# The down projection of an encoder's MLP by Strassen's scheme, its weight differences on GpSimd

## The chip, the cores and the metric

The kernel runs on one core of a Trainium2 chip. A core has five engines that run side by side, each with its own queue of instructions in a fixed order: TensorE (PE) multiplies matrices, VectorE (DVE), ScalarE (ACT) and GpSimd (POOL) work elementwise, SyncE (SP) issues transfers. The metric is the device time of one execution in microseconds, as the median of several runs. Operands lie in SBUF, the matmuls' sums in PSUM, which has eight banks of 128 x 512 fp32 numbers.

## The reference

Two layers of an encoder on 512 tokens of width 1024. Each layer has a token mixer (two kinds of attention, gated and projected) and then an MLP:

```
mod = silu(c) @ ada_w[l] + ada_b[l]            # 6 x 1024 numbers: shifts, scales, gates
h = rms_norm(x, norm_mlp_g[l]) * (1.0 + scale_f) + shift_f
x = x + gate_f * (jnp.square(jax.nn.relu(h @ w_mlp_up[l])) @ w_mlp_down[l])
```

The up projection is 1024 to 4096, the down projection 4096 to 1024. All is fp32.

## The kernel before

**Precision.** Every fp32 operand is split into a high part, in the matmul's format `fp32r`, and a low part, the rest. A product is three matmuls into the same sum (`mm3`, L265): high by high, high by low, low by high. A weight block of 128 x 1024 comes by DMA into a tile `raw`; `split_w` (L249) makes its high part `wh` on ACT (a copy that rounds) and its low part `wl` on DVE (`raw` minus `wh`). There are four `raw` buffers (`rawp`, L51) and five pairs of `wh` and `wl` (`wp`, L52). Larger tiles of 4 KB a partition share 24 buffers (`bigp`), 512-wide scratch six.

**The MLP.** The hidden 4096 columns are worked on in eight chunks (the loop `for fc`, L965) of four blocks of 128. `up_part` (L946) multiplies one block's weights with the normed activations `hF` for all 512 tokens: 8 x 3 = 24 matmuls of 512 columns into a bank. Then ACT takes the relu `r`, DVE makes the square `q` from the bank and `r`, ACT and DVE split `q` into the two halves of a tile `uT`. After four blocks the chunk's down products follow: for each half `cc` of the 1024 output columns and each of the four token tiles `t`, 4 x 3 = 12 matmuls into a bank; DVE multiplies it with the gate row `gf` into `d`, and POOL adds `d` to the residual tile `x1[t]` (in the last chunk DVE adds). The first three blocks (`EARLY`) are begun ahead of the loop, half of their tokens at a time.

**The conditioning of the next layer.** While layer 0's chunks run, `ada` (L141) forms the 48 blocks of `mod` for layer 1: a 128 x 1024 block of `ada_w` into a `raw` buffer, multiplied with the broadcast `cbc` and summed along its rows by one DVE instruction (profile: `raw<-raw,cbc,colt`). Eight are called behind each of the first six chunks. With `pool_` set, POOL multiplies (`raw<-raw,cbc`), ACT sums, and a small DVE addition (the closure `add`) closes.

**Order.** In the chunk loop no order is written out: a planner sorts the instructions by the order of the program text and by what it takes to be ready, with times that it estimates, and assigns buffers as they come free. On the chip each engine then runs its own list in that order and waits where something isn't ready. In other stages (the last output projection and the beginning of the up blocks, the last half chunk of layer 0, attention) `order(True)` keeps the order of the text.

**Banks.** `acc()` takes PSUM banks in turn from two pools, `accp` (2) and `ssp` (3). Two more (`tpp`) serve transposes, one (`pvp`) attention.

In the profile nearly every instruction has line L81, that of a helper; so groups are told apart by tile names. Names there merge the two parts of a matmul's operands: `acc<-wh,uT` holds high by high and low by high.

Of the kernel before, what the change touches and what calls it, by code (L numbers as in the profile page):

```python
# [10 lines left out]
F32 = mybir.dt.float32  # L11
R32 = mybir.dt.float32r
BF = mybir.dt.bfloat16
I32 = mybir.dt.int32
AF = mybir.ActivationFunctionType
OP = mybir.AluOpType
AX = mybir.AxisListType

DEPTH = 2
# [4 lines left out]
NFF = 32  # L24
FCH = 4
# [16 lines left out]
def trunk(ctx, tc, x, c, pos, cols, rows, ada_w, w_qkv, w_gate, w_ba, w_bb, w_out, w_up, w_down, out):  # L42
# [8 lines left out]
    rawp = pool("raw", 4)  # L51
    wp = pool("w", 5)  # L52
    halfp = pool("half", 10)
    pp = pool("p", 2)
    sp = pool("scr", 2)
    accp = pool("acc", 2, PS)
    ssp = pool("ss", 3, PS)
    tpp = pool("tp", 2, PS)
    pvp = pool("pv", 1, PS)
    dram = pool("dram", 1, bass.MemoryType.DRAM)  # L60

    def nosync(after, before):
        tc.add_manual_dep(after.ins, before.ins.name,
                          mybir.DependencyInfo(mybir.DependencyClass.NoSync,
                                               mybir.DependencyReason.DATA), reason="order")
# [23 lines left out]
    T_, V_, S_, G_ = Ordered(nc.tensor), Ordered(nc.vector), Ordered(nc.scalar), Ordered(nc.gpsimd)  # L89
    E_ = Ordered(nc.sync)  # L90
    matmul = T_.matmul
    transpose = T_.transpose
    big = lambda shape, dt, name: bigp.tile(shape, dt, name=name, tag="big")
    turns = [0]

    def acc(wide=True):
        turns[0] += 1
        if wide and turns[0] % 5 >= 2:
            return ssp.tile([128, 512], F32, name="acc", tag="s")
        return accp.tile([128, 512], F32, name="acc", tag="acc")  # L100
# [40 lines left out]
    def ada(l, j, far=False, pool_=False):  # L141
        raw = big([128, D], F32, "raw") if far else rawp.tile([128, D], F32, name="raw", tag="raw")
        E_.dma_start(raw, ada_w[l, j])
        m, bias = modT[l][:, j:j + 1], adab[l][:, j:j + 1]

        def add():
            S_.activation(raw, raw, AF.Copy, accum_out=m)
            V_.tensor_add(m, m, bias)

        if pool_:  # L150
            G_.tensor_mul(raw, raw, cbc)
            return add
        else:
            ins = V_.tensor_tensor_reduce(raw, raw, cbc, 1.0, bias, OP.mult, OP.add, m)
            if floor[0] is not None:
                nosync(ins, floor[0])
# [105 lines left out]
                                           op0=OP.mult, op1=OP.subtract)  # L262
        return hi, lo

    def mm3(o, sh, sl, mh, ml, start, stop):  # L265
        matmul(o, sh, mh, start=start, stop=False)
        matmul(o, sh, ml, start=False, stop=False)
        matmul(o, sl, mh, start=False, stop=stop)

    def rsq(o, ms):  # L270
        G_.tensor_scalar(ms[:, 0:1], ms[:, 0:1], ms[:, 1:2], EPS, op0=OP.add, op1=OP.add)
# [47 lines left out]
    def affine(l, m):  # L319
        aT = small([128, KT], "aT")  # L320
        sc = modT[l][:, 24 * m + 8:24 * m + 16]
        V_.scalar_tensor_tensor(aT, sc, 1.0, gnorm[l, m], op0=OP.add, op1=OP.mult)
        return aT

    def grow(l, m):
        g = pp.tile([128, D], F32, name="grow", tag="p")
        before = T_.last
        for q in range(2):
            tp = tps()
            for k in range(4):  # L330
                j = 24 * m + 16 + 4 * q + k
                ins = transpose(tp[:, k], modT[l][:, j:j + 1].to_broadcast([128, 128]), ident)
                if before is not None:
                    nosync(ins, before)
            S_.activation(g[:, 512 * q:512 * q + 512], tp.rearrange("p a b -> p (a b)"), AF.Copy)
        return g
# [255 lines left out]
    EARLY = 3  # L592
# [14 lines left out]
    def prepare(l):  # L607
        hT = []
        return hT, [qkv(l, p, int(p < 6), hT) for p in range(NB_Q)]
# [104 lines left out]
    for l in range(DEPTH):  # L714
# [161 lines left out]
        x1 = {}  # L876
        zT = []
        wb = None
        for j in range(KT):
# [11 lines left out]
            wh, wl = split_w(w_ba[l, j], scale=sg[:, l:l + 1])  # L891
# [5 lines left out]
            zb = sp.tile([128, 512], F32, name="zb", tag="f512", bufs=6)  # L897
# [12 lines left out]
        up = {}  # L910
        ms = {}
        for cc in range(2):
            w = [split_w(w_out[l, cc, i], spare=cc == 1 and i == 0) for i in range(4)]
# [5 lines left out]
            for t in range(NT):  # L919
                if cc == 0:  # L920
                    x1[t] = load_x(t, xsrc)
                ps = acc()
                tk = slice(128 * t, 128 * t + 128)
                for kt in range(KT):
                    wh, wl = w[kt // 2]
                    cw = slice(512 * (kt % 2), 512 * (kt % 2) + 512)
# [19 lines left out]
        def up_part(j, lo, hi):  # L946
            if j not in up:
                up[j] = [split_w(w_up[l, j])]
            if lo == 0:
                up[j].append(acc())  # L950
            (wh, wl), ps = up[j]
            hs = slice(lo, hi)
            for kt in range(KT):
                kc = slice(128 * kt, 128 * kt + 128)
                mm3(ps[:, hs], wh[:, kc], wl[:, kc], hF[kt][0][:, hs], hF[kt][1][:, hs], kt == 0, kt == KT - 1)
            return ps
# [5 lines left out]
        order(False)  # L962
        if l + 1 < DEPTH:
            x2d = dram.tile([NT, 128, D], F32, name=f"x2d{l}")
        for fc in range(NFF // FCH):  # L965
            uT = []
            last = fc == NFF // FCH - 1
            for f in range(FCH):
                j = fc * FCH + f
                ps = up_part(j, 256, 512) if j < EARLY else up_part(j, 0, 512)  # L970
                r = sp.tile([128, 512], F32, name="r", tag="f512", bufs=6)
                q = sp.tile([128, 512], F32, name="q", tag="f512", bufs=6)
                u = big([128, 2, 512], R32, "uT")
                S_.activation(r, ps, AF.Relu)
                V_.scalar_tensor_tensor(q, ps, 0.0, r, op0=OP.max, op1=OP.mult)
                S_.activation(u[:, 0], q, AF.Copy)
                V_.tensor_sub(u[:, 1], q, u[:, 0].bitcast(F32))
                uT.append(u)
            if fc == 0:
                gf = grow(l, 1)  # L980
            if last and l + 1 < DEPTH:
                nxt = prepare(l + 1)
                for i in range(2):
                    nxt[1][0]["load"](i, True)
            for cc in range(2):
                w = [split_w(w_down[l, fc, cc, i]) for i in range(2)]
                if last and l + 1 < DEPTH and cc == 0:
                    nxt[1][0]["load"](2)
                ahead = last and cc == 1 and l + 1 < DEPTH
                if ahead:  # L990
                    pairs = halves(nxt[0])
                    aT = affine(l + 1, 0)
                    norms = []
                    order(True)
                    nxt[1][0]["load"](3)
                for t in range(NT):
                    tk = slice(128 * t, 128 * t + 128)
                    d = sp.tile([128, 512], F32, name="d", tag="f512", bufs=6)
                    final = last and l == DEPTH - 1 and cc == 1 and t == NT - 1
                    for lo, hi in ((0, 256), (256, 512)) if final else ((0, 512),):  # L1000
                        ps = acc()[:, lo:hi]
                        for f in range(FCH):
                            wh, wl = w[f // 2]
                            cw = slice(512 * (f % 2) + lo, 512 * (f % 2) + hi)
                            mm3(ps, uT[f][:, 0, tk], uT[f][:, 1, tk], wh[:, cw], wl[:, cw], f == 0, f == FCH - 1)
                        xs = slice(512 * cc + lo, 512 * cc + hi)
                        V_.tensor_mul(d[:, lo:hi], ps, gf[:, xs])
                        (V_ if last else G_).tensor_add(x1[t][:, xs], x1[t][:, xs], d[:, lo:hi])
                        if last and l == DEPTH - 1:
                            E_.dma_start(out[t, :, xs], x1[t][:, xs])  # L1010
                    if last and l + 1 < DEPTH and cc == 0:
                        ms[t] = msp.tile([128, 2], F32, name="ms2", tag="ms")
                        square(x1[t], ms[t], 0)
                    if ahead:
                        norms.append(norm(l + 1, 0, t, x1[t], ms[t], aT, pairs))
                        if t > 1:
                            norms[t - 2][2]([0])
                        norms[t][0]()
                        E_.dma_start(x2d[t], x1[t])
                        if t > 0:  # L1020
                            norms[t - 1][1]()
                        if t > 1:
                            norms[t - 2][2]([1])
                if ahead:
                    norms[3][1]()
                    early = {1 + i: norms[2 + i][2] for i in range(2)}
            if l + 1 < DEPTH and not last:
                for i in range(8 if fc < 6 else 0):
                    ada(l + 1, fc * 8 + i)


_ORDER = ["x", "c", "pos", "cols", "rows", "ada_w", "w_qkv", "w_gate", "w_ba", "w_bb", "w_out", "w_up",
# [64 lines left out]
```

## Time and profile before

| what | value |
|---|---|
| median of three runs | 1906.12 us (1905.95 to 1906.64) |
| the profiled execution | 1906.47 us, its span 1904.7 us |
| granted TensorE clock, mean | 0.996 |
| busy: PE, DVE, ACT, POOL | 99%, 64%, 46%, 27% |
| matmuls | 10144 |
| moved by DMA | 212.11 MB, 111 GB/s |
| chunk loop of layer 0 | about 632 to 980 us |
| chunk loop of layer 1 | about 1556 us to the end |

The span goes from the first to the last instruction. Busy shares are means over all stages. A matmul is recorded with its whole way through the array, so that matmuls next to each other overlap in the record. A row of a timeline gives start in us, duration in us, engine, line, operation, output and inputs, and in brackets how long the engine was idle before and what ended that. A row of windows gives the window, its length, and then the busy us of PE, of PE's weight loads, of DVE, ACT and POOL (number of instructions in brackets), the granted clock, the DMA share and GB/s. A row of a group ends with its total busy time, the mean ns of one, and the idle time of its engine before it.

### The profile page before, as it was taken

Reading aid. Unit: us, or ns where it says so; the run is one execution under the profiler, and the core shown is the slowest. Engines: PE = TensorE matmul, PEld = TensorE weight load, DVE = VectorE, ACT = ScalarE, POOL = GpSimd, SP = SyncE. Lnnn points to the kernel's source line nnn. Section 1 sums busy time; section 2 is a strip of 40 time slices with the busy share of each in tenths; the row PEclk is TensorE's granted clock in tenths of the full one; section 3 lists DMA queues with packets and bytes.
Section 4 is the critical chain, followed back from the end, with each engine's and each line's share of the span. In section 5 each row is a group of like instructions: output and inputs, shape, how many; then the busy total and the mean of one; then the engine's idle time right before and its main releaser. Section 6 shows DMA issues by size and latency. Waiting matters only on the chain.

```text
span 1904.7 us, 27604 instructions
## 1 busy us (share of the span) xinstructions
PE 1876.4 (99%) x10144; PEld 1657.7 (87%) x10144; DVE 1218.8 (64%) x2519; ACT 878.6 (46%) x1927; POOL 510.1 (27%) x535
## 2 busy tenths in 40 slices
PE   7999999999999999999999999999999999999999
PEld 5999999998878888888889999999888888888887
DVE  8776678877586766775487566878543464445444
ACT  5555566766234323223355555676653353222221
POOL 4332324331121222222233232334100102223330
PEclk8999999999999999999999999999999999999999
DMA  8321121224583655664232121112143333323321
GB/s 301 132 68 59 51 59 43 70 67 155 189 275 122 208 181 198 195 204 151 70 111 75 59 67 42 59 43 70 56 122 89 133 94 106 100 89 100 100 89 56
DMA packets 63640, 212.11 MB, mean 111 GB/s; under 512 B 7185, under 2 KB 7569, under 8 KB 63506
## 3 DMA queue, kind: packets, MB, share of 16 engines
q1 hardware_dynamic: 63218, 210.27, 34.3%
q8 instruction: 80, 1.31, 0.3%
q14 instruction: 54, 0.44, 0.1%
q10 hardware_dynamic: 288, 0.09, 0.0%
HBM read 205.09 MB, written 5.24 MB: 110 GB/s over the span
## 4 chain that ended last, share of the span: by engine, by line
PE 80%; DVE 8%; ACT 4%; DMA 3%; issue 2%; POOL 2%; SPq 0%; ACTq 0%; DVEq 0%; POOLq 0%
PE acc L81 68%; PE tp L81 4%; PE s L81 4%; PE pv L81 3%; DVE wl L81 2%; PE pvb L81 2%; ACT wh L81 1%; DVE raw L81 1%; DMA raw<-in_w_ba 1%; POOL rs L81 1%; DVE T L81 1%; DVE ms L81 1%; DVE kl L81 1%; ACT e L81 1%; DMA raw<-in_w_gate 1%
## 5 line engine op out<-in xcount | busy, mean ns | idle before, releaser
L81 PE MATMUL acc<-wh,hT 128*128 128x384 f32 x1792 | 516.6, 346 | 6.5 <-ACT hT L81 4.8
L81 DVE TENSOR_TENSOR wl<-raw,wh 128x1024 fp32r<-128x1024 f32 (+1 forms) x292 | 343.4, 1183 | 262.2 <-ACT wh L81 260.4
L81 PE MATMUL acc<-hT,wh 128*128 128x512 f32 (+1 forms) x1632 | 481.1, 378 | 0.0
L81 ACT ACTIVATE wh<-raw 128x1024 fp32r<-128x1024 f32 (+1 forms) x292 | 281.0, 978 | 371.6 <-PE acc L81 337.3
L81 PEld LDWEIGHTS acc<-hT,wh 128*128 128x128 f32 x1632 | 298.9, 188 | 54.7
L81 PEld LDWEIGHTS acc<-wh,hT 128*128 128x128 f32 x1792 | 329.6, 188 | 12.5 <-ACT hT L81 6.0
L81 PE MATMUL acc<-wh,uT 128*128 128x512 f32 (+1 forms) x1032 | 318.2, 388 | 0.1
L81 PE MATMUL acc<-hT,wl 128*128 128x512 f32 (+1 forms) x816 | 307.9, 378 | 1.1 <-DVE wl L81 1.1
L81 PE MATMUL acc<-wl,hT 128*128 128x384 f32 x896 | 302.5, 338 | 0.9 <-DVE wl L81 0.8
L81 POOL TENSOR_TENSOR xt<-xt,d 128x512 f32<-128x512 f32 x112 | 170.2, 1547 | 446.9 <-DVE d L81 446.9
L81 POOL TENSOR_TENSOR rs<-ms,half_neg 128x4 f32<-128x4 f32 (+1 forms) x128 | 123.4, 964 | 473.8 <-DVE ms L81 472.6
L81 PEld LDWEIGHTS acc<-wh,uT 128*128 128x128 f32 x1032 | 193.3, 188 | 40.1 <-DVE d L81 0.5
L81 PE MATMUL acc<-wl,uT 128*128 128x512 f32 (+1 forms) x516 | 199.1, 387 | 0.0
L81 PEld LDWEIGHTS acc<-hT,wl 128*128 128x128 f32 x816 | 153.5, 188 | 30.1 <-DVE wl L81 1.9
L81 PEld LDWEIGHTS acc<-wl,hT 128*128 128x128 f32 x896 | 169.3, 189 | 5.1 <-DVE wl L81 2.5
L81 DVE TENSOR_TENSOR d<-acc,grow 128x512 f32<-128x512 f32 (+1 forms) x145 | 95.2, 681 | 86.8 <-PE acc L81 71.9
L81 DVE CUSTOM_DVE_ANT_0 raw<-raw,cbc,colt 128x1024 f32<-128x1024 f32 x94 | 123.5, 1324 | 38.5 <-DMA raw<-in_ada_w 38.4
L81 ACT ACTIVATE p<-s,nm 128x512 f32<-128x512 f32 x128 | 86.9, 684 | 72.6 <-DVE nm L81 72.6
L81 PEld LDWEIGHTS acc<-wl,uT 128*128 128x128 f32 x516 | 96.9, 188 | 19.7
L81 ACT ACTIVATE uT<-q 128x512 fp32r<-128x512 f32 x64 | 40.4, 632 | 121.0 <-DVE q L81 121.0
L81 DVE TENSOR_REDUCE nm<-s 128x1 f32<-128x512 f32 x128 | 82.2, 683 | 19.7 <-PE s L81 19.7
L81 PE MATMUL s<-k,q 128*128 128x512 f32 (+1 forms) x224 | 84.7, 386 | 2.1 <-DVE n L81 2.1
(146 smaller groups left out, 2641.8 us busy)
## 6 DMA issues: line engine op xcount, KB each, us to landing
raw<-in_ada_w SPq DMA_DIRECT2D x96, 512.0 KB, 4.5
raw<-in_w_qkv SPq DMA_DIRECT2D x112, 384.0 KB, 3.1
raw<-in_w_up SPq DMA_DIRECT2D x64, 512.0 KB, 4.2
raw<-in_w_down SPq DMA_DIRECT2D x64, 512.0 KB, 3.6
raw<-in_w_gate SPq DMA_DIRECT2D x32, 512.0 KB, 3.6
raw<-in_w_ba SPq DMA_DIRECT2D x16, 512.0 KB, 4.1
raw<-in_w_out SPq DMA_DIRECT2D x16, 512.0 KB, 3.7
xt<-in_x SPq DMA_DIRECT2D x8, 512.0 KB, 6.1
```

The source lines that it names most:

```text
L81: ins = f(*a, **k)
```

## The change

In the first seven of the eight chunks the down product, 512 tokens by 512 hidden columns by 1024 outputs, is cut in two in each direction, and the eight products of halves become seven by Strassen's scheme in Winograd's form. For activations a11, a12, a21, a22 (token half by hidden half) and weights r11 to r22:

- s1 = a21 + a22, s2 = s1 - a11, s3 = a11 - a21, s4 = a12 - s2 (DVE);
- t1 = r12 - r11, t2 = r22 - t1, t3 = t2 - r11, t4 = r21 - t2, in place in r12, r12, r11, r21 (POOL, 128 x 1024 each);
- the products in order, with P1 to P7 the names used below: P1 = a11 r11, P2 = a12 r21, P3 = s1 t1, P4 = s2 t2, P5 = s4 r22, P6 = s3 t3, P7 = a22 t4.

A product fills two banks (one for each 128 tokens of the half) with 12 matmuls. P4, P6 and P7 go on summing in the banks of P1, P5 in those of P3. After each product `take` adds its two banks to two of the eight tiles `y7` (DVE; in the first chunk the first time for each of the four quarters is a copy on ACT). So `d` and the addition into `x1` are gone from these chunks; ahead of the last chunk DVE multiplies the eight `y7` with the gate row and POOL adds them to `x1`. The last chunk runs as before.

Each operand is split where it is used: `usplit` (ACT, DVE, 512 columns, seven times for four) and `wsplit` (ACT, DVE, 1024, seven for four). r11 and r12 lie in large buffers, r21 and r22 in `raw` buffers. The up blocks other than the first three and the last four take their banks from `tpp` and `pvp` (`ubank`). In layer 0 seven `ada` are called behind each of the seven chunks (six behind the seventh) in place of eight behind six; three in seven go by way of POOL.

```
-            if lo == 0:
-                up[j].append(acc())
+                up[j].append(acc() if j < EARLY or j >= NFF - FCH else ubank())
...
+        def ubank():
+            upturn[0] += 1
+            pool_, tag = ((tpp, "tp"), (tpp, "tp"), (pvp, "pv"))[upturn[0] % 3]
+            return pool_.tile([128, 512], F32, name="acc", tag=tag)
+
+        def product(banks, u, w, start):
+            wh, wl = w
+            for i, ps in enumerate(banks):
+                for k in range(2):
+                    tk = slice(256 * k + 128 * i, 256 * k + 128 * i + 128)
+                    cw = slice(512 * k, 512 * k + 512)
+                    mm3(ps, u[:, 0, tk], u[:, 1, tk], wh[:, cw], wl[:, cw], start and k == 0, k == 1,
+                        skip_group_check=not start)
+
+        def chunk7(fc, ys):
+            q = [big([128, 2, 512], F32, "q7") for _ in range(2)]
+            for f in range(FCH):
...
+                S_.activation(r, ps, AF.Relu)
+                V_.scalar_tensor_tensor(q[f // 2][:, f % 2], ps, 0.0, r, op0=OP.max, op1=OP.mult)
+            a11, a21 = q[0][:, :, 0:256], q[0][:, :, 256:512]
+            a12, a22 = q[1][:, :, 0:256], q[1][:, :, 256:512]
+            s1, s2, s3, s4 = (sp.tile([128, 2, 256], F32, name="s7", tag="f512", bufs=6) for _ in range(4))
+
+            def usplit(a):
+                u = big([128, 2, 512], R32, "uT")
+                hi, lo = (u[:, i].rearrange("p (a b) -> p a b", a=2) for i in range(2))
+                S_.activation(hi, a, AF.Copy)
+                V_.tensor_sub(lo, a, hi.bitcast(F32))
+                return u
+
+            def wsplit(raw):
+                hi, lo = (wp.tile([128, 1024], R32, name=n_, tag=n_) for n_ in ("wh", "wl"))
+                S_.activation(hi, raw, AF.Copy)
+                V_.tensor_sub(lo, raw, hi.bitcast(F32))
+                return hi, lo
+
+            r11, r12 = (big([128, 1024], F32, "raw") for _ in range(2))
+            r21, r22 = (rawp.tile([128, 1024], F32, name="raw", tag="raw") for _ in range(2))
+            for r, (j, k) in ((r11, (0, 0)), (r21, (1, 0)), (r12, (0, 1)), (r22, (1, 1))):
+                E_.dma_start(r, w_down[l, fc, k, j])
+
+            def take(y, ps):
+                if fc == 0 and y not in ys:
+                    ys[y] = [halfp.tile([128, 512], F32, name="y7", tag="half") for _ in range(2)]
+                    for yt, b in zip(ys[y], ps):
+                        S_.activation(yt, b, AF.Copy)
+                else:
+                    for yt, b in zip(ys[y], ps):
+                        V_.tensor_add(yt, yt, b)
+
+            bank = lambda pool_, tag: [pool_.tile([128, 512], F32, name="acc", tag=tag) for _ in range(2)]
+            xb = bank(ssp, "s")
+            product(xb, usplit(a11), wsplit(r11), True)
+            take((0, 0), xb)
+            zb = bank(accp, "acc")
+            product(zb, usplit(a12), wsplit(r21), True)
+            take((0, 0), zb)
+            V_.tensor_add(s1, a21, a22)
+            G_.tensor_sub(r12, r12, r11)
+            yb = bank(accp, "acc")
+            product(yb, usplit(s1), wsplit(r12), True)
+            take((1, 1), yb)
+            V_.tensor_sub(s2, s1, a11)
+            G_.tensor_sub(r12, r22, r12)
+            product(xb, usplit(s2), wsplit(r12), False)
+            take((0, 1), xb)
+            V_.tensor_sub(s4, a12, s2)
+            product(yb, usplit(s4), wsplit(r22), False)
+            take((0, 1), yb)
+            V_.tensor_sub(s3, a11, a21)
+            G_.tensor_sub(r11, r12, r11)
+            product(xb, usplit(s3), wsplit(r11), False)
+            take((1, 1), xb)
+            G_.tensor_sub(r21, r21, r12)
+            product(xb, usplit(a22), wsplit(r21), False)
+            take((1, 0), xb)
+
+        ys = {}
         for fc in range(NFF // FCH):
             uT = []
             last = fc == NFF // FCH - 1
+            if not last:
+                chunk7(fc, ys)
+                if fc == 0:
+                    gf = grow(l, 1)
+                if l + 1 < DEPTH:
+                    for i in range(7 * fc, min(7 * fc + 7, 48)):
+                        add = ada(l + 1, i, False, i % 7 in (1, 3, 5))
+                        if add is not None:
+                            add()
+                continue
+            for (i, cc), y2 in sorted(ys.items()):
+                for k, y in enumerate(y2):
+                    xs = slice(512 * cc, 512 * cc + 512)
+                    V_.tensor_mul(y, y, gf[:, xs])
+                    G_.tensor_add(x1[2 * i + k][:, xs], x1[2 * i + k][:, xs], y)
...
-            if l + 1 < DEPTH and not last:
-                for i in range(8 if fc < 6 else 0):
-                    ada(l + 1, fc * 8 + i)
```

More of the change, by code (lines that the diff above doesn't have):

```diff
@@ L263, in split_w, with mm3 @@
         return hi, lo
[L265 to L268, printed above, removed]
+    def mm3(o, sh, sl, mh, ml, start, stop, **more):
+        matmul(o, sh, mh, start=start, stop=False, **more)
+        matmul(o, sh, ml, start=False, stop=False, **more)
+        matmul(o, sl, mh, start=False, stop=stop, **more)
     def rsq(o, ms):
@@ L964, in trunk @@
             x2d = dram.tile([NT, 128, D], F32, name=f"x2d{l}")
+        upturn = [0]
+        def ubank():
[10 more added lines that the diff above has]
+                        skip_group_check=not start)
@@ new lines, in chunk7 @@
+        def chunk7(fc, ys):
+            q = [big([128, 2, 512], F32, "q7") for _ in range(2)]
+            for f in range(FCH):
+                j = fc * FCH + f
+                ps = up_part(j, 256, 512) if j < EARLY else up_part(j, 0, 512)
+                r = sp.tile([128, 512], F32, name="r", tag="f512", bufs=6)
+                S_.activation(r, ps, AF.Relu)
[52 more added lines that the diff above has]
+            take((1, 0), xb)
@@ L978, in trunk @@
                 uT.append(u)
-            if fc == 0:
-                gf = grow(l, 1)
             if last and l + 1 < DEPTH:
```

## The prediction

> **What bounds the kernel now.** I read the busy table first, then the chain that ended last, then windows over the MLP of each layer, then the timelines of VectorE (DVE) and GpSimd (POOL) inside them.
>
> ```profile
> span 1904.7 us, 27604 instructions
> PE 1876.4 (99%) x10144; PEld 1657.7 (87%) x10144; DVE 1218.8 (64%) x2519; ACT 878.6 (46%) x1927; POOL 510.1 (27%) x535
> PE 80%; DVE 8%; ACT 4%; DMA 3%; issue 2%; POOL 2%; SPq 0%; ACTq 0%; DVEq 0%; POOLq 0%
> 652.11 310.39 PE acc L81 x1368
> 719.50:763.00 43.50, 43.50 (x194) 36.02 (x193) 29.91 (x41) 12.64 (x16) 12.02 (x8) 1.00 0.59 193
> 1655.50:1699.00 43.50, 20.62 (x24) 1.00 0.32 98
> ```
>
> The chain is TensorE (PE). In the chunk loop of layer 0 it runs 310.39 us without a break: 1368 matmuls, so one every 310.39 / 1368 = 0.2269 us. A chunk has 192 of them (96 up, 96 down), 43.5 us; the window of that length shows PE busy for all of it, DVE (third number) 29.9 us, ScalarE (ACT) 12.6, POOL 12.0. The last row is DVE alone in a chunk of layer 1: 20.6 us, since only layer 0 also works on the conditioning (`ada`) of the layer after it. So a chunk is PE's, with DVE two thirds full in layer 0 and half full in layer 1. The granted clock is 1.00.
>
> ```profile
> L81 PE MATMUL acc<-wh,uT 128*128 128x512 f32 x435 | 134.3, 389 | 0.0
> L81 POOL TENSOR_TENSOR xt<-xt,d 128x512 f32<-128x512 f32 x51 | 77.9, 1555 | 188.4 <-DVE d L81 188.4
> L81 ACT ACTIVATE wh<-raw 128x1024 fp32r<-128x1024 f32 x53 | 56.1, 1059 | 128.5 <-PE acc L81 118.5 <-DMA raw<-in_w_up 9.9
> L81 ACT ACTIVATE uT<-q 128x512 fp32r<-128x512 f32 x28 | 17.7, 632 | 76.8 <-DVE q L81 76.8
> L81 ACT ACTIVATE r<-acc 128x512 f32<-128x512 f32 x28 | 16.2, 579 | 0.0
> L81 DVE TENSOR_TENSOR wl<-raw,wh 128x1024 fp32r<-128x1024 f32 x53 | 70.3, 1326 | 36.3 <-ACT wh L81 36.2
> ```
>
> These groups are of the loop of layer 0 (660 to 960 us). A matmul's duration, 389 ns, is not its price: neighbours overlap, and the price is the 0.227 us between starts.
>
> **The change on PE.** Per Strassen chunk, 8 groups of 12 down matmuls become 7 products of 12: 12 × 0.227 = 2.72 us less, 40.8 us in place of 43.5. Over 7 chunks and 2 layers that is 168 matmuls, 38.1 us, the most that the change can bring. The page Trainium Kernel Development and Optimization of the Trainium skill, section Performance Expectations, says that matmul busy time misleads because matmuls are pipelined. Priced by busy time the change would bring 168 × 0.389 = 65.4 us; the rule tells against that, and the starts in this trace agree with it. The 12 that stay in a product have the same shapes.
>
> **What DVE gets.** In a busy stretch an instruction's price is the distance between starts (the first row is from the start of the kernel, the others from a chunk of layer 0):
>
> ```profile
> 31.50 0.14 DVE L81 TENSOR_TENSOR modT<-modT,colt 128x1 f32<-128x1 f32 x1
> 769.84 1.28 DVE L81 CUSTOM_DVE_ANT_0 raw<-raw,cbc,colt 128x1024 f32<-128x1024 f32 x1
> 771.04 0.08 DVE L81 DVE_READ_ACCUMULATOR2_ANT modT<- 128x1 f32 x1
> 774.71 0.69 DVE L81 TENSOR_TENSOR uT<-q,uT 128x512 fp32r<-128x512 f32 x1
> 775.31 0.68 DVE L81 SCALAR_TENSOR_TENSOR q<-acc,r 128x512 f32<-128x512 f32 x1
> 775.91 1.22 DVE L81 TENSOR_TENSOR wl<-raw,wh 128x1024 fp32r<-128x1024 f32 x1
> 777.04 0.68 DVE L81 TENSOR_TENSOR uT<-q,uT 128x512 fp32r<-128x512 f32 x1
> 777.65 1.22 DVE L81 TENSOR_TENSOR wl<-raw,wh 128x1024 fp32r<-128x1024 f32 x1
> 778.93 2.48 DVE L81 TENSOR_TENSOR d<-acc,grow 128x512 f32<-128x512 f32 x4
> ```
>
> A 128x512 operation is 0.60, a weight's low half (`wl`) 1.13, an `ada` 1.20, `d` 0.60. Before, a chunk of layer 1 has 8 `wl`, 4 `q`, 4 `uT`, 8 `d`: 9.0 + 9.6 = 18.6 (the window shows 20.6 with overlaps). After: 11 `wl` (4 up, 7 for the products) 12.4; 4 `q` 2.4; 7 low halves of the activations 4.2; s1 to s4 2.4; 7 takes of two banks 14 × 0.60 = 8.4. Sum 29.8 us for layer 1. Layer 0 adds 4 `ada` on DVE, 4.8, and three small additions (`modT`, 0.14 at most) that close those on POOL, some 0.3: 34.9. The takes have no row; `d` is nearest (one PSUM and one SBUF input, 128x512), so 0.60; at a `wl`'s price per element it would be 0.57. In chunk 0 eight takes are ACT copies, 4.8 less on DVE.
>
> **What POOL gets, and what that does to DVE.** It loses the 8 additions into `x1` of each chunk and gains four 128x1024 weight differences; in layer 0 also three `ada` products of that size.
>
> ```profile
> 27.23 2.40 POOL L81 TENSOR_TENSOR raw<-raw,cbc 128x1024 f32<-128x1024 f32 x1
> 27.07 4.50 DVE L81 TENSOR_TENSOR wl<-raw,wh 128x1024 fp32r<-128x1024 f32 x2 [0.26 <-ACT wh L81]
> 37.19 2.97 POOL L81 TENSOR_TENSOR raw<-raw,cbc 128x1024 f32<-128x1024 f32 x1 [7.57 <-DMA raw<-in_ada_w]
> 38.26 2.46 DVE L81 TENSOR_TENSOR hT<-h,hT 128x512 fp32r<-128x512 f32 x1 [0.35 <-ACT hT L81]
> 1672.03 8.52 POOL L81 TENSOR_TENSOR xt<-xt,d 128x512 f32<-128x512 f32 x6 [28.42 <-DVE d L81]
> 1671.20 2.48 DVE L81 TENSOR_TENSOR d<-acc,grow 128x512 f32<-128x512 f32 x4
> 1673.59 2.07 DVE L81 TENSOR_TENSOR wl<-raw,wh 128x1024 fp32r<-128x1024 f32 x1
> ```
>
> One POOL product of 128x1024 takes 2.40. Two `wl` beside it took 4.50 where 1.13 + 1.22 = 2.35 is normal: they lost 2.15 of its 2.40, a share of 0.89. The next one stretched a 0.69 `hT` to 2.46. The four `d` beside POOL's additions kept 0.62 each, and the `wl` behind them went from 1.22 to 2.07. So an operation with both inputs in SBUF waits for POOL's running one; one that reads PSUM does not. In a whole chunk of before, that 0.85 is all that I find lost, of 8 × 8.52 / 6 = 11.4 us: a share f of 0.07, because DVE mostly waited for PE then.
>
> POOL's new work is 4 × 2.40 = 9.6 us a chunk in layer 1 and 7 × 2.40 = 16.8 in layer 0. DVE's time a chunk is its own plus f times that.
> - Layer 1: 29.8 + 9.6 f. Even f = 0.89 gives 38.3, under PE's 40.8. DVE is not the bound; what is left are waits inside the products. P6 and P7 write the same banks: P7's first matmul needs the take of bank 0, and PE comes back to it after six matmuls, 1.36 us; a take is 0.68, but it queues behind a 1.2 us `wl` if one is ahead, itself perhaps held by POOL; behind the take stand the low halves that the next products wait for. P3 takes over P2's banks likewise. Between none (matmuls of the next chunk's up fill in; its three banks are separate) and 2.7 us a chunk (the gain), nearer the first since PE ran its whole chunk unbroken before: 0.8. Gain 7 × (2.72 − 0.8) = 13.4 us.
> - Layer 0: 34.9 + 16.8 f. It stays under 40.8 only for f < 0.35 and breaks even with 43.5 at f = 0.51. With DVE full, POOL's time is free only beside its PSUM reads, 2.4 + 8.4 = 10.8 us of the 34.9: f is at least 1 − 10.8 / 16.8 = 0.36. Of 44 operations 18 read PSUM, mostly in pairs of 1.2; a POOL start that falls anywhere meets some 0.5 us of such reads (my estimate): f = 1 − 0.5 / 2.4 = 0.8. I take 0.7, between that and the good placing, nearer the crowded rows: 46.7 us, 3.2 more than before. Chunks 1 to 6: 6 × 3.2 = +19.2. Chunk 0 (34.9 − 4.8 + 11.8 = 41.9): −1.6.
>
> The page SBUF — State Buffer of the Trainium skill, section Who interferes with whom, states that a DVE instruction with two SBUF inputs and a GpSimd one that reads SBUF block each other for the whole instruction. Taken as f = 1 its sum would be 34.9 + 16.8 = 51.7 us in chunks 1 to 6, about 1940 in all; the rows give 0.89 at most, and the same section lets PSUM readers pass, as the `d` rows show.
>
> **Covered at nothing.** ACT in layer 0: 11 `wh` × 1.06 + 7 high halves × 0.63 + 4 `r` × 0.58 + 3 `ada` sums × 1.05 (`raw<-raw` below) = 21.5 of 40.8; a high half stands ahead of each product (0.63 and 1.06), so out of turn it would show as part of the 0.8. The SP queue issues 15 transfers a chunk for 16.
>
> ```profile
> raw<-in_ada_w SPq DMA_DIRECT2D x96, 512.0 KB, 4.5
> raw<-in_w_up SPq DMA_DIRECT2D x64, 512.0 KB, 4.2
> L81 ACT ACTIVATE raw<-raw 128x1024 f32<-128x1024 f32 x2 | 2.1, 1053 | 1.9 <-POOL raw L81 1.9
> ```
>
> But r21 and r22 sit in two of the four `raw` buffers from loading to P7 and P5; 11 other weights a chunk share what is left, at 4.2 to 4.5 landing plus 1.2 to 3.5 in use, about 7 us each: 77 us in 2 to 4 buffers. It fits in layer 0 with little to spare; with no cover an up weight would come a landing, some 4 us, late. The end of the scheme (8 multiplications, 0.60; 8 POOL additions, 1.42, 11.4 us) runs beside the up half of the last chunk, 96 matmuls or 21.8 us of PE; uncovered it would cost 11.4 us a layer. The other banks for up (`ubank`) add no instruction; the first chunk's gate row takes two of them for its transposes, under 1 us beside PE's own work.
>
> **Sum.** 1906.47 us is the profiled execution (span 1904.7); 1906.47 + 19.2 − 1.6 − 13.4 = 1910.7. Its time is 0.35 us over the median, so 1910.3; I say 1911, 0.25% slower.
>
> **Rivals.**
> - *The port is cheap* (faster): the differences fall beside takes and idle stretches, f = 0.4. Layer 0's chunks are 41.6: 6 × −1.9 − 2.7 = −14.1, with layer 1 −13.4: 1879. For it: 0.07 in the chunk of before. Against: DVE had 13.6 us free there. It decides below f = 0.63, where the total falls under 1902.7.
> - *Even*: f between 0.63 and 0.69, the layers cancel: 1906.
> - *The products starve* (slower): P6 to P7 and the chain POOL difference, `wh`, `wl`, product cost 2.7 us a chunk in both layers; layer 1 gives nothing and layer 0 loses as forecast: 1906.5 + 19.2 − 1.6 = 1924. For it: four new operations hang in one row behind POOL. Against: five weight buffers let a split run five groups ahead.
>
> **How the numbers follow.** A measurement of this kernel tells 0.2% (3.8 us) from no change. Forecast (f from 0.69 to 0.89, 1910 to 1932): 0.37. Port cheap: 0.36. Even: 0.17. Starved: 0.10. Faster 0.36, same 0.17, slower 0.47. As both signs hold most of it, the range goes from 1880 (f = 0.4) to 1934 (f = 0.89 and some waits); the likeliest case alone is 1910 to 1932.
>
> **What would show it.** Chunks of layer 1 near 41.6 us and PE above 97% busy there; chunks 1 to 6 of layer 0 at 45 to 48 with DVE over 90% busy and PE waiting for `wl` or for the takes; `wl` in layer 0 with a mean far over 1.33 us; POOL's 128x1024 operations at 2.4 or more. Wrong if layer 0's chunks are under 43 (f overrated), if layer 1's are not shorter than 43.5 (waits underrated), or if up weights wait for their transfers.

## The result, and the profile after

| | before | after |
|---|---|---|
| median | 1906.38 us (4 runs) | 2091.48 us (4 runs, 2090.64 to 2094.95) |
| ratio | | 1.0973, 95% interval 1.0954 to 1.0992 |
| span of the profiled execution | 1904.7 us | 2089.8 us |
| matmuls | 10144 | 9976 |
| mean granted TensorE clock | 0.996 | 0.958 |

The change made the kernel 9.7% slower: 185 us where I had forecast 5. From the page of the changed kernel, the span, the busy table, the chain by engine and two groups:

```profile
span 2089.8 us, 27422 instructions
PE 1909.5 (91%) x9976; PEld 1659.5 (79%) x9976; DVE 1459.3 (70%) x2722; ACT 972.2 (47%) x2069; POOL 567.2 (27%) x516
PE 40%; DVE 12%; DMA 2%; issue 2%; ACT 2%; POOL 2%; ACTq 0%; DVEq 0%; POOLq 0%
L81 PE MATMUL acc<-wh,uT 128*128 128x512 f32 (+1 forms) x920 | 342.0, 441 | 139.4 <-ACT wh L81 51.3
L81 POOL TENSOR_TENSOR raw<-raw 128x1024 f32<-128x1024 f32 x56 | 148.2, 2656 | 340.6 <-DMA raw<-in_w_down 193.8
```

The 168 matmuls are gone as forecast, yet PE's busy time rose, since a matmul on `uT` now takes 441 ns in the mean for 389, and PE was idle for 139.4 us ahead of these. The chain holds less of PE and more of DVE. From the first down matmul of layer 0 to that of layer 1 the kernel takes 1056.1 us for 935.9, and from there to the end 395.3 for 330.6: 120 us were lost in layer 0, 65 in layer 1.

Where, is shown by the waits of PE: what it waited for, total us, times, longest. In the chunks of layer 0 (690 to 1060 us):

```profile
PE acc L81 <- ACT wh L81: 43.9, 10, 10.1
PE acc L81 <- DVE y L81: 21.6, 7, 4.8
PE acc L81 <- DVE wl L81: 11.0, 8, 2.3
PE acc L81 <- DVE uT L81: 9.4, 3, 4.3
```

and in those of layer 1 (from 1720 us on):

```profile
PE acc L81 <- DVE uT L81: 22.1, 5, 4.4
PE acc L81 <- DVE y L81: 18.8, 6, 3.4
PE acc L81 <- ACT wh L81: 3.0, 1, 3.0
```

Windows of one chunk of each layer, in the columns of the prediction's first fence:

```profile
882.60:944.20 61.60, 47.54 (x180) 36.94 (x180) 46.63 (x53) 20.53 (x30) 17.42 (x7) 0.88 0.37 128
1823.70:1875.90 52.20, 44.58 (x182) 35.75 (x181) 37.08 (x41) 17.23 (x22) 10.59 (x4) 0.93 0.25 81
```

A chunk of layer 1 lasts 52.2 us for 43.5; the window of layer 0 shows 61.6. DVE is busy 37.1 of 52.2 (71%) and 46.6 of 61.6 (76%): no engine is full, PE waits.

**One chunk of layer 1, from its timeline.** POOL's three last differences run without a pause; the DVE rows under it are in DVE's order, most of them 512 wide. Then PE's two waits of this chunk.

```profile
1857.11 8.27 POOL L81 TENSOR_TENSOR raw<-raw 128x1024 f32<-128x1024 f32 x3 [12.96 <-DVE wl L81]
1855.82 1.22 DVE L81 TENSOR_TENSOR wl<-raw,wh 128x1024 fp32r<-128x1024 f32 x1
1856.95 0.68 DVE L81 TENSOR_TENSOR s<-s,q 128x512 f32<-128x512 f32 x1
1857.55 2.83 DVE L81 TENSOR_TENSOR uT<-q,uT 128x512 fp32r<-128x512 f32 x1
1860.31 2.86 DVE L81 TENSOR_TENSOR uT<-s,uT 128x512 fp32r<-128x512 f32 x1
1863.09 2.84 DVE L81 TENSOR_TENSOR s<-q,s 128x512 f32<-128x512 f32 x1
1865.85 0.68 DVE L81 TENSOR_TENSOR s<-q 128x512 f32<-128x512 f32 x1
1860.44 0.74 PE L81 MATMUL acc<-wh,uT 128*128 128x512 f32 x2 [4.43 <-DVE uT L81]
1867.78 0.72 PE L81 MATMUL acc<-wh,uT 128*128 128x512 f32 x1 [3.19 <-DVE y L81]
```

From 1857.55 to 1865.85 DVE does three operations in 8.30 us that cost 1.80 alone: it lost 6.50 us to three POOL operations of 2.40, 7.2 in all (beside DVE they took 8.27). They are the splits of a12 for P2 and of s1 for P3, and s4. PE's first wait is for the split of a12; its second for a take, which stands behind them all in DVE's list and must read P2's bank before P3 writes there. PE's list has no other work in between. And behind each wait its matmuls start every 0.43 us, not 0.227. Three windows, behind the first wait, behind the second, and later (the granted clock is the third number from the end):

```profile
1861.10:1864.40 3.30, 3.30 (x9) 2.22 (x7) 3.30 (x2) 0.00 (x0) 3.30 (x2) 0.50 0.00 0
1867.90:1871.30 3.40, 3.40 (x9) 2.62 (x10) 3.40 (x5) 2.57 (x4) 0.00 (x0) 0.50 0.00 0
1872.00:1890.00 18.00, 18.00 (x81) 14.92 (x80) 14.06 (x18) 4.73 (x5) 0.00 (x0) 1.00 0.53 159
```

So the clock fell to half for some 3.4 us behind each wait, and the waits were paid a second time. The page TensorE: Matmul & The Clock Gate of the Trainium skill, section HAM oscillation, describes this: a wait across a window of about 3.4 us halves PE's clock until it has been busy again. The trace agrees in the half and in the 3.4 us, but a wait shorter than such a window, 3.19 us here, was enough (more on this in the last section). Adding up the distances between PE's starts over the chunk (1823.7 to 1875.9 us): 180 matmuls at the full rate are 40.8 us, waits 8.2 us, the excess of the slow matmuls 3.2 us, together 52.2.

**One chunk of layer 0.** The row of PE is the first matmul of a chunk's P1; those of SP and ACT come just ahead of it.

```profile
945.80 0.80 PE L81 MATMUL acc<-wh,uT 128*128 128x512 f32 x1 [6.96 <-ACT wh L81]
915.91 22.02 SPq L81 DMA_DIRECT2D raw<-in_ada_w  x7
938.03 0.85 SPq L81 DMA_DIRECT2D raw<-in_w_down  x2
936.04 1.06 ACT L81 ACTIVATE raw<-raw 128x1024 f32<-128x1024 f32 x1 [6.54 <-POOL raw L81]
943.17 1.06 ACT L81 ACTIVATE raw<-raw 128x1024 f32<-128x1024 f32 x1 [4.97 <-POOL raw L81]
944.70 1.99 ACT L81 ACTIVATE wh<-raw 128x1024 fp32r<-128x1024 f32 x2
```

SP needs 22 us to issue seven conditioning loads, one at a time as buffers come free (r21 and r22, issued ahead of them, hold two of the four), and only then issues the loads of r11 and r12, which P1 and t1 need first. ACT stands in its fixed order at the conditioning's sums, 6.54 and 4.97 us, each behind a POOL product that stands behind a load; the `wh` for P1 comes behind them at 944.70, and PE has waited 6.96 us. Most of this wait is the late load: in the trace r11, issued at 938.03, had landed only at 943.20; the other 1.5 us are ACT's order.

### The profile page after: what moved, and what is told of

It reads as the page before. It is cut to its first block, busy times and chain, and to the rows that moved or that the text cites. A ratio compares the mean times of both kernels' runs of the same rounds, so it can differ in the third digit from the quotient of the medians.

```text
span 2089.8 us, 27422 instructions
## 1 busy us (share of the span) xinstructions
PE 1909.5 (91%) x9976; PEld 1659.5 (79%) x9976; DVE 1459.3 (70%) x2722; ACT 972.2 (47%) x2069; POOL 567.2 (27%) x516
## 4 chain that ended last, share of the span: by engine, by line
PE 40%; DVE 12%; DMA 2%; issue 2%; ACT 2%; POOL 2%; ACTq 0%; DVEq 0%; POOLq 0%
PE acc L81 34%; DVE uT L81 3%; DVE wl L81 3%; DMA raw<-in_ada_w 2%; PE tp L81 2%; DVE s L81 2%; DVE y L81 2%; PE s L81 2%; PE pv L81 1%; POOL raw L81 1%; PE pvb L81 1%; ACT raw L81 0%; POOL rs L81 0%; ACT wh L81 0%; DVE raw L81 0%
## 5 line engine op out<-in xcount | busy, mean ns | idle before, releaser
L81 DVE TENSOR_TENSOR wl<-raw,wh 128x1024 fp32r<-128x1024 f32 (+1 forms) x334 | 396.8, 1200 | 122.1 <-ACT wh L81 121.5
L81 PE MATMUL acc<-wh,uT 128*128 128x512 f32 (+1 forms) x920 | 342.0, 441 | 139.4 <-ACT wh L81 51.3
L81 ACT ACTIVATE wh<-raw 128x1024 fp32r<-128x1024 f32 (+1 forms) x334 | 320.8, 984 | 249.1 <-PE acc L81 158.1
L81 POOL TENSOR_TENSOR raw<-raw 128x1024 f32<-128x1024 f32 x56 | 148.2, 2656 | 340.6 <-DMA raw<-in_w_down 193.8
L81 DVE CUSTOM_DVE_ANT_0 raw<-raw,cbc,colt 128x1024 f32<-128x1024 f32 x73 | 110.1, 1518 | 72.6 <-DMA raw<-in_ada_w 72.4
L81 DVE TENSOR_TENSOR y<-y,acc 128x512 f32<-128x512 f32 x180 | 119.8, 678 | 40.1 <-PE acc L81 39.8
L81 POOL TENSOR_TENSOR raw<-raw,cbc 128x1024 f32<-128x1024 f32 x23 | 56.2, 2445 | 220.4 <-DMA raw<-in_ada_w 194.2
L81 DVE SCALAR_TENSOR_TENSOR q<-acc,r 128x512 f32<-128x512 f32 x64 | 43.7, 687 | 85.2 <-ACT r L81 85.2
```

Of the source, the lines that this page charges most:

```text
L81: ins = f(*a, **k)
```

## The experiments

Lengths are of one chunk, the distance between starts of every 84th matmul on `uT`, as the median of chunks 1 to 6. (In layer 1 of the changed kernel such starts lie at 1852.2 and 1904.4 us, for one; the window from 1823.7 to 1875.9 us above is a period of the same length.) The kernel before has 43.5, and 40.8 would be PE without a wait.

| kernel | total us | layer 0 | layer 1 |
|---|---|---|---|
| after | 2091.5 | 59.0 | 52.2 |
| diffs_on_dve | 2038.2 | 55.8 | 48.6 |
| no_diffs | 2003.1 | 53.0 | 47.7 |
| diffs_early | 2076.7 | 61.5 | 48.0 |
| ada_on_dve | 2069.8 | 58.0 | 52.3 |
| no_ada | 2038.5 | 52.3 | 52.8 |
| up_ahead | 2014.2 | 53.6 | 45.2 |

**Off GpSimd: diffs_on_dve, no_diffs, diffs_early.** In the first all four differences change engine, in the second they are dropped.

```
-            G_.tensor_sub(r12, r12, r11)
+            V_.tensor_sub(r12, r12, r11)          # diffs_on_dve, and so for all four
```

> The four weight differences of a chunk run on DVE (4 x 1.13 us more for it), none on POOL. Theory A (the port): in a chunk of layer 1 three POOL differences back to back stretch three 512-wide DVE operations, on which products P3 and P4 hang, from 0.68 to about 2.85 each; without them PE's 8.2 us of waits fall to about 3 and the 3.2 us of half-clock matmuls behind them to about 1: chunk 45 us for 52.2, layer 0's 54 for 61, in all 2091 - 7 x 7 - 7 x 7 = about 1993 us. Theory B (the chain of sums, splits and takes is too long for two products whatever POOL does): DVE only gets more work ahead of P3, chunks of layer 1 at 52 to 56 us, in all 2091 to 2140. Theory C (DVE is full in layer 0, as I had forecast): layer 1 as in A, layer 0's chunks no shorter than 60.

> The four weight differences are left out (products P3, P4, P6, P7 take the plain r12, r12, r11, r21), everything else stays: the time of the scheme with its differences for nothing. A: waits of 1 to 2 us a chunk are left in layer 1, chunk 42 to 43 us; layer 0 keeps what the conditioning's POOL products do, 50 to 55; in all about 1960. B: 50 us or more in layer 1, about 2075 in all.

1 run each, 53 and 88 us faster than after. Theory A's direction holds: giving DVE 4.5 us more work and POOL none shortens a chunk of layer 1 by 3.6 us. But the 48.6 us are neither A's 45 nor B's 52, and with the differences for nothing 47.7 are left, 6.9 over PE's 40.8, where A had 1 to 2. What is left is B's, and no_diffs shows it, in DVE's rows at the start of a chunk's products, and PE's wait there:

```profile
1786.02 0.69 DVE L81 TENSOR_TENSOR y<-y,acc 128x512 f32<-128x512 f32 x1 [1.38 <-PE acc L81]
1786.62 1.22 DVE L81 TENSOR_TENSOR wl<-raw,wh 128x1024 fp32r<-128x1024 f32 x1
1787.76 0.68 DVE L81 TENSOR_TENSOR y<-y,acc 128x512 f32<-128x512 f32 x1
1788.35 1.22 DVE L81 TENSOR_TENSOR wl<-raw,wh 128x1024 fp32r<-128x1024 f32 x1
1789.49 0.69 DVE L81 SCALAR_TENSOR_TENSOR q<-acc,r 128x512 f32<-128x512 f32 x1
1790.89 0.79 PE L81 MATMUL acc<-wh,uT 128*128 128x512 f32 x1 [3.78 <-ACT uT L81]
```

The last up block's square `q`, ready to run from about 1785.8 on, stands behind two takes and two low halves in DVE's list. Then come its split and P2. P1, 2.7 us from 1784.23 on, covers only the first microsecond of that. Whether another order in DVE's list (`q` ahead of the takes) would be enough, no run shows.

```
+            t1, t3, t4 = (big([128, 1024], F32, "t7") for _ in range(3))
+            G_.tensor_sub(t1, r12, r11)           # diffs_early: all four here, behind the loads;
+            G_.tensor_sub(r12, r22, t1)           # t3 and t4 likewise
```

> The four differences stay on POOL but are written in the text ahead of the products, into buffers of their own (t1, t3, t4; t2 in r12), so that none waits for a split of another. POOL's work and the port's are the same, only the place moves. A: the three differences leave the moment at which DVE forms s1, s2 and their splits; chunk of layer 1 43 to 45 us, in all about 1990 with layer 0's conditioning as it is. B: no change, 52 us and 2091. If POOL's differences only wait for the later r21 and r22 transfers and collide somewhere else: 47 to 52.

Layer 1 fell to 48.0, not to A's 43 to 45, but as with no POOL work in the chain. POOL's work is that of after, so it was the place (with buffers of its own) and not the amount that cost 4.2 us a chunk there. Layer 0 did not gain (61.5): its differences now run behind the conditioning's products in POOL's list (951.40 and 955.17 us in one chunk), and PE waits 13.2 us ahead of the first down matmul of the layer.

**The conditioning: ada_on_dve, no_ada, before_ada7.**

```
-                        add = ada(l + 1, i, False, i % 7 in (1, 3, 5))
+                        add = ada(l + 1, i)       # ada_on_dve; no_ada drops the loop
```

> The change, but all seven conditioning blocks a chunk on DVE, none by way of POOL and ACT. Theory D (in layer 0 POOL's first difference and ACT's weight copies stand in their queues behind the conditioning's POOL products and ACT sums, which wait for transfers): PE's waits for the weight copies, 3.8 and 7.0 us a chunk, go; layer 0's chunks 61 to about 52 like layer 1's, in all 2091 - 7 x 9 = about 2028 us, layer 1 unchanged. Theory C (DVE full): DVE has 3 x 1.2 - 0.4 = 3.2 us more a chunk, layer 0's chunks 61 to 64, in all 2091 to 2115.

> The change without the 48 conditioning blocks of layer 0's chunks (that part of the computation is left out, layer 1's modulation is set to a constant). Theory D (the conditioning, in the queues of SP, POOL and ACT ahead of the products' weights, makes up all that layer 0 loses beyond layer 1): layer 0's chunks 61 to 52, as in layer 1; in all 2091 - 7 x 8.7 = about 2030 us. Rival (layer 0's chunks lose for a reason of their own, buffers or the larger share of GpSimd): above 55 us a chunk, over 2050 us.

Without it layer 0's chunks last 52.3 us, as in layer 1, and 53 us of the 185 are gone, all in layer 0: theory D's place was right. What is left over the kernel before, 67 us in layer 0 and 66 in layer 1, is the products' own loss. ada_on_dve gained 22 us, a third of what D promised (10 of them in the first chunk, which the median leaves out); so the way over POOL and ACT is a part of it, and the other 31 us are the blocks themselves, by whatever route. My theory C, a full DVE, had this run no faster; it was faster.

> The kernel before with the change's handling of the conditioning alone: seven blocks behind each of seven chunks, three in seven by way of POOL and ACT. If this route alone holds up POOL's and ACT's queues: layer 0's chunks 43.5 to 46 or more, in all 1920 to 1930. If it hurts only together with the products' differences and splits, as I think (before, nothing on POOL is needed by PE): 43.5 us a chunk, 1906 us.

1931.6 us, 1 run: this expectation was wrong. The change's handling of the conditioning alone, on the kernel before, costs 25 us. PE's waits in its layer 0:

```profile
PE acc L81 <- ACT uT L81: 14.4, 6, 2.8
```

and what stands ahead of one of them:

```profile
776.00 2.34 DVE L81 CUSTOM_DVE_ANT_0 raw<-raw,cbc,colt 128x1024 f32<-128x1024 f32 x1 [1.56 <-DMA raw<-in_ada_w]
778.28 3.41 DVE L81 TENSOR_TENSOR wl<-raw,wh 128x1024 fp32r<-128x1024 f32 x1
778.15 2.45 POOL L81 TENSOR_TENSOR raw<-raw,cbc 128x1024 f32<-128x1024 f32 x1 [0.89 <-DMA raw<-in_ada_w]
782.32 0.63 ACT L81 ACTIVATE uT<-q 128x512 fp32r<-128x512 f32 x1 [3.87 <-DVE q L81]
783.00 0.50 PE L81 MATMUL acc<-wh,uT 128*128 128x512 f32 x1 [2.21 <-ACT uT L81]
```

Six waits of 2 to 3 us, one a chunk, with slow matmuls behind five of them; together these are the 25 us. All six have the same rows ahead of them. Two POOL products of the conditioning stretch DVE's own conditioning operation to 2.3 to 2.4 us for 1.28, and a weight's low half to 3.4 for 1.22; in the rows above that is 3.2 us lost, more than PE's wait. The block's square `q` stands behind both in DVE's list, and ACT and then PE wait for it. So it is the shared port again, and it isn't needed that POOL works for PE, as I had thought.

**Work for PE beside the chain: up_ahead, and then less of the scheme.**

```
             take((0, 0), xb)
+            for j in range(FCH * (fc + 1), FCH * (fc + 1) + 1):   # 2 in the kernels named "two"
+                up_part(j, 0, 512, True)                          # its bank from ubank()
             zb = bank(accp, "acc")
```

(The lines in `up_part` that go with it are left out here.)

> Differences on DVE, and the first up block of the next chunk stands in the text behind P1, ahead of P2, so that PE has 5.4 us of work while the last block's square goes through the sums and splits. Theory B' (what is left in layer 1 with the differences off POOL, some 5 us of waits and 2 us of half clock a chunk, is the chain from the last up block to P2 and P3, with nothing on PE beside it): layer 1's chunks 48.4 to 42 or 43, layer 0's 56 to 50; in all 2038 - 14 x 6 = about 1955 us. Rival (DVE's fixed list puts other work ahead of that chain, by more than 5 us, or the weight buffers are too few for one more): 47 or more, above 2015 us.

2014.2 us: 24 us from diffs_on_dve, where 83 were expected; layer 1 to 45.2 and not 42, layer 0 to 53.6 and not 50. B' is right in direction, but 5.4 us of cover was too little.

> Strassen's scheme in layer 1 alone, with the differences on DVE and the up block ahead; layer 0 is the kernel before. By B' seven chunks of 42 to 43 us for 43.5, and about 5 us lost at the layer's start: 1906 - 7 x 1 + 5 = 1897 to 1910 us. By the rival 1906 + 7 x 4 + 5 = about 1939 us.

> As the last, but the differences stay on POOL, early in the text and in buffers of their own. If POOL's work, once out of the chain's way, costs DVE less than doing the differences itself: one us a chunk less than with DVE, 1890 to 1905 us. If the port still bites in the chain: 1 to 3 us a chunk more.

1921.3 and 1916.0 us (1 run each; before 1906.6 beside them), above what was expected: chunks of 44.1 and 43.6 us, a first one with 8 and 12 us of waits and slow matmuls, and in layer1_only a seventh of 48.5. Early differences on POOL were the cheaper by 5 us. Leaving the first chunk out too:

> Strassen's scheme in layer 1, chunks 1 to 6 alone (chunk 0, whose start lost 12 us in the last run, and layer 0 as before), the differences early on POOL, and two up blocks of the next chunk behind P1 (10.9 us of PE work). By B' the waits of 1.5 to 2 us a chunk shrink to under 0.5 and with them the half clock: 41.3 us a chunk for 43.5, 1906 - 6 x 2.2 + 2 = about 1895 us. Rival (five pairs of weight buffers are too few for two blocks more, so the products' weights come late): 44 to 46 us a chunk, 1909 to 1921.

> The same with the differences on DVE. If the port is what still slows the low halves of the weights ahead of the chain (three in 6.1 us for 3.5 in the run with early POOL differences), this is the faster by about 0.5 us a chunk, 1892; if DVE's own 4.5 us more count for more, slower, 1898 to 1905.

> Chunks 1 to 6 of layer 1, the differences early on POOL, one up block ahead: the chunks of the last run of this form, 43.7 us, without its first one: 1916 - 10 = about 1906 us, even with before. Under 1900 if the first chunk's wait had also upset those behind it.

| kernel | median us (runs) | ratio to before (1906.13, 13 runs), 95% interval |
|---|---|---|
| six_early_two | 1898.03 (4) | 0.9955 (0.9938 to 0.9972) |
| six_dve_two | 1899.30 (4) | 0.9962 (0.9947 to 0.9977) |
| six_early_one | 1907.49 (10) | 1.0008 (0.9998 to 1.0017) |

With two up blocks behind P1 the scheme pays, within 3 us of the expected 1895: six chunks of layer 1 save 8.1 us, 1.35 each, half of the 2.72 that a chunk has in it. One block is even with before, so the length of the cover decides. Of six_early_two, PE's waits in layer 1 from 1555 us on:

```profile
PE acc L81 <- DVE wl L81: 2.8, 3, 1.3
PE acc L81 <- DVE y L81: 1.8, 6, 0.8
```

a window of some two chunks:

```profile
1700.00:1783.00 83.00, 81.32 (x355) 66.09 (x354) 69.65 (x81) 33.88 (x44) 21.81 (x9) 1.00 0.31 102
```

and rows of DVE and POOL in it:

```profile
1739.90 7.91 DVE L81 TENSOR_TENSOR wl<-raw,wh 128x1024 fp32r<-128x1024 f32 x3
1747.74 0.68 DVE L81 SCALAR_TENSOR_TENSOR q<-acc,r 128x512 f32<-128x512 f32 x1
1738.80 6.80 POOL L81 TENSOR_TENSOR t<-raw 128x1024 f32<-128x1024 f32 x2
```

DVE is busy 84% of the window here, fuller than in the changed kernel's 71%, and PE 98%, at full clock. The rows show the port still at work, three low halves in 7.91 us for some 3.5 beside two POOL differences, and the square `q` behind them; but PE now has up matmuls until 1751.27 and does not wait. Whether POOL or DVE forms the differences makes no difference that these runs can tell.

**All three undone in both layers.**

> The form of six_early_two in both layers (chunks 1 to 6, differences early on POOL, two up blocks ahead), with the 48 conditioning blocks of layer 0's chunks left out of the computation. If the three causes are all: layer 0 gains what layer 1 gained, 8 us each, 1906 - 16 = about 1890 us. If layer 0 has a loss of its own: over 1898.

> The same with the conditioning as in the kernel before (eight a chunk behind six chunks, on DVE). If its amount is too much beside the scheme (DVE 29.8 + 9.6 + POOL's share, and 16 blocks a chunk through two to four raw buffers): layer 0's chunks 46 to 50, in all 1910 to 1935 us. If only its route over POOL and ACT hurt: near 1890 to 1895.

both_no_ada 1890.5 us (2 runs, ratio 0.9913, 0.9885 to 0.9942): layer 0 gains what layer 1 does, 8 us each, and no loss of another kind is left. (The kernel before was not run without its conditioning; its PE was busy all through these chunks.) both_ada8 1940.1 (2 runs, 1.0174, 1.0144 to 1.0203), 5 us over the end of what I had put for too large an amount: all of the conditioning on DVE, as before the change, still costs 50 us beside the scheme. So layer 0 has room for both by neither route that was run. How its cost splits between DVE's time and the buffers no run here tells apart.

## Why the prediction was wrong

- **PE's saving.** Right: 168 matmuls fewer, priced by the distance between starts, 0.227 us; a busy time of 389 ns would have promised too much.
- **The port.** Right in kind, and in size where POOL's operations meet DVE's: 6.50 / 7.2 = 0.90, for the rows' 0.89. But f was to be a share of all of POOL's time in a chunk, and as such it is 6.5 / 9.6 = 0.68 in this chunk of layer 1, and 8.3 / 16.8 = 0.49 in the window of layer 0 (the sum of what its stretched DVE rows lost), for the 0.7 taken. Put into the sum, 0.49 would have made layer 0's chunks about as long as before. Wrong is what it costs: I turned it into DVE's total per chunk and compared that with PE's; it acted by delaying operations that PE waited for.
- **The waits inside the products, 0.8 us a chunk.** This is the step that failed. In layer 1 they measured 8.2 us a chunk and the slow matmuls behind them 3.2, for my 0.8; with "the gain", 2.7, as the upper end I had left no room for a loss in layer 1 at all. I had set a take of 0.68 against six matmuls. One of the two waits is where I had looked, at P3 taking over P2's banks, but its take stood behind a whole row of sums and splits; the other, for the split of a12, I had not seen. Both hang on the chain from the last up block over `q`, sums and splits to P2 and P3, in DVE's fixed order, with POOL on it. Seven chunks at 8.7 us over before are 61 us, and layer 0 without the conditioning loses as much again (no_ada).
- **"With DVE full" in layer 0.** Failed: DVE was 76% busy. 46.7 us was forecast, 59.0 measured; that the sign was right there is luck.
- **Covered at nothing.** The `raw` buffers I called tight, and priced at nothing. ACT's "21.5 of 40.8" counted its time and not its order. The conditioning, with which both of these come, cost 53 us (after against no_ada).
- **The clock.** Not in the prediction: I took matmuls at 0.227 us whatever PE had waited.
- **The rivals.** "The products starve" named the mechanism nearest to the truth, and bounded it by the gain, 2.7 us a chunk; waits and slow matmuls together, 11.4, were four times that. Its argument against, five weight buffers ahead, spoke of the weights and not of the activations.

## What to carry to other kernels

Shares of busy time say whether an engine can keep up, not whether what it owes comes in time: where a step makes an engine's output depend on the last thing computed, follow that one chain in the queues' order, and ask what the bounding engine runs meanwhile. Place the partner's work on a shared port (here GpSimd's on VectorE's) outside the chain, and give the matmul engine independent matmuls beside it, ahead in the program order; a wait of a few us is also paid again at a lower clock.

## What the runs showed of the hardware that I had not expected

- At half clock, matmuls of 512 columns start every 0.43 us. In the traces the granted clock is 1.0 or 0.5, in stretches of 3.41 us or multiples of it, and a wait's length alone does not tell which. (A window below that is a little off such a stretch shows 0.99 or 0.51.) Four windows of before_ada7, around a wait of PE of 2.75 us (the first two) and one of 1.94 (the third):

```profile
685.10:688.50 3.40, 1.71 (x8) 1.09 (x6) 3.40 (x2) 0.00 (x0) 2.06 (x1) 1.00 0.57 218
688.50:691.90 3.40, 2.34 (x10) 1.85 (x11) 2.77 (x7) 3.02 (x5) 0.00 (x0) 1.00 0.82 263
732.90:736.30 3.40, 1.47 (x7) 0.80 (x6) 2.77 (x5) 1.64 (x4) 0.04 (x1) 0.99 0.91 329
736.30:739.70 3.40, 3.40 (x10) 2.63 (x9) 3.33 (x6) 2.09 (x4) 0.00 (x0) 0.51 0.74 280
```

  The longer wait is spread over two stretches, with PE busy for 1.71 and 2.34 us, and the clock stays full. The shorter one lies within one, which leaves 1.47 us, and the next is at half. In four traces (after, no_ada, diffs_on_dve and before_ada7, from 600 us on) 75 stretches at full clock are followed by one at half; PE was busy for at most 1.64 us in each of them, and for at least 1.53 in every one that is followed by full clock.
- A short DVE operation beside back-to-back POOL operations of 2.40 us takes 2.83 to 2.86 us for 0.68, and each operation of DVE meets one of POOL: they take turns. Where the order of the lists puts such a row into a chain that PE waits for, this is the price that counts.
- The page Perfetto Trace Analysis of the Trainium skill, section Optimizing Scalar/DVE Operations, warns that moving work between GpSimd and VectorE may not help because of their shared port. These runs agree: back on DVE the differences cost 53 us less in the changed kernel, and where a chain no longer met them, 1898.0 against 1899.3 us, the engine did not matter.
